# Pinning the pieces of a state-space set-up to places in a feed-forward layer

## The chip, the cores and the metric

The kernel runs on one core of a Trainium2 chip. The metric is device time in microseconds (us) for one execution. The engines are TensorE (PE in the profile: matmuls; PEld is its weight load), VectorE (DVE), ScalarE (ACT), GpSimd (POOL) and SyncE (SP), whose queue issues nearly all DMAs.

## The reference

One inference step of a two-layer decoder for 512 prompt tokens and 64 sample tokens, 576 columns in all. Layer 0 is dilated window attention and a gated feed-forward layer, layer 1 a state-space (S5) layer and another feed-forward layer. Cut to what the change is about:

```python
def swiglu(h, w_gate, w_up, w_down):
    return (jax.nn.silu(h @ w_gate) * (h @ w_up)) @ w_down

def ssm_layer(h, state0, w_in, a_re, a_im, log_dt, b_re, b_im, c_re, c_im, d_skip, w_glu):
    u = (h @ w_in).astype(f32)
    lam = lax.complex(a_re, a_im)
    dt = jnp.exp(log_dt)[:, None]
    abar = jnp.exp(lam * dt)
    bbar = ((abar - 1.0) / lam)[..., None] * lax.complex(b_re, b_im)
    cmat = lax.complex(c_re, c_im)
    ...   # scan over time: x = abar * x + bbar u; y = Re(C x) + D u
    g = jax.nn.gelu(y)
    val, gate = jnp.split(g @ w_glu, 2, axis=-1)
    return val * jax.nn.sigmoid(gate), h_last

x = x + out                       # mixer of the layer
x = x + swiglu(rmsnorm(x), ...)   # feed-forward of the layer
```

Everything in `ssm_layer` that doesn't depend on `h` (the powers of `abar`, `bbar`, and the matrices that turn eight time steps into one matmul) can be made ahead. That is the state-space set-up. The model width is 1024, the feed-forward width 2816, and there are 64 groups of 64 states.

## The kernel before

All matmuls are done as three: weights and activations are split into a high part that the matmul takes exactly and a low rest, and hi x hi, hi x lo and lo x hi are added. For each weight piece of 512 x 256, `fetch_w` (L85 to L89) loads it into one of four `raw` buffers, ScalarE makes `whi` (L99) and DVE makes `wlo = raw - whi` (L100), each with two buffers. `mark[0]` keeps the latest of these DVE instructions and `pem[0]` the latest matmul, as the code is traced. With every fetch, `pace` also issues one copy of a piece of the old key/value cache to the output, of about 1 MB (L83), and keeps these copies in program order on SyncE.

`ffn` (layer 0's feed-forward) works through the 2816 columns in three thirds of 4, 4 and 3 column blocks of 256. A column block takes a gate product (two weight pieces), the product with the norm on DVE (L1078), Silu on ScalarE, a second product with the norm on GpSimd (L1080, into `gt`), an up product (two pieces), and the product of both on DVE (L1085), which is split into `hh` and `hl`. After each third come four blocks of the down product, of two pieces each, added into `xT` (L1091). After each weight piece `gemm` calls `tick`. That takes the state-space set-up, a Python generator, one `yield` further. So `ffn` has 16 + 8, 16 + 8 and 12 + 8, or 68 places for it.

The set-up, `ssm_setup`, has these pieces (their places in the kernel before):

- loads of its constants (place 1), queued behind the last load of the output projection;
- on DVE: an exponential (3), sine and cosine (4, 5), the powers `Ar`, `Ai` (6), the factor `af` (8), `Bz` and four transposes on PE (10); then `at` is written to `a_scr` in device memory (12);
- on GpSimd: powers up to 63, `ee` (13 to 18), `E63` (21), written to `e_scr` (23);
- for each of eight families f: loads of `af` (from `a_scr`), `bt` and `C` (place 25 for f = 0); six products on GpSimd into `vx` (26 + 4f); four products on DVE for each half of `af` with `bt` (27 + 4f and 28 + 4f, L1513 to L1516); the write of `af` to `w_scr` (28 + 4f); the loads for f + 1, eight small matmuls into `aux`, DVE's copies into `kk`, and writes of `vx` (29 + 4f); the write of `kk` to `t_scr` (30 + 4f);
- loads of the finished constants `Wc`, `Ec`, `Tc`, `Vc` for families 0 to 3 (place 59).

A place is only where a piece stands in the program. The order on each engine is made by a planner, which simulates the whole program with durations of its own: an instruction whose inputs it takes to be there, and whose engine is free, goes into the order, and among several the one that stands first in the program. An engine then runs its list strictly in that order. So an instruction of a late place can stand ahead of one of an early place where the planner took the engine to be idle. Two things bind it: `tc.issue_after(i)` puts each instruction of its block that runs on `i`'s engine behind `i` in that engine's order, and `tc.keep_in_program_order` keeps such instructions of one engine in program order among themselves. Before the change the set-up uses the first for its constants' loads and for its matmuls on PE (behind `pem`), and the second not at all.

The tiles `af`, `bt`, `vx`, `kk` of the families have one buffer each, `C` two. The load of `af` for f + 1 so waits for the write of family f's `af` to `w_scr`. The pool of the families' tiles takes the place of the pool of `ee`, which in turn takes that of the first pieces.

Of the kernel before, what the change touches and what calls it, by code (L numbers as in the profile page):

```python
# [8 lines left out]
F32 = mybir.dt.float32  # L9
# [41 lines left out]
def _build(nc, tc, A, es):  # L51
# [51 lines left out]
    pem = [None]  # L103
# [943 lines left out]
def ffn(nc, tc, A, L, nin, nout, fill):  # L1047
# [20 lines left out]
    with ExitStack() as es:  # L1068
        hp = es.enter_context(pool("hp", bufs=9))
        wk = es.enter_context(pool("wkf", bufs=2))  # L1070
        for c0, c1 in THIRDS:
            h = {}
            for c in range(c0, c1):
                pg = gemm(lw("ffn_w_gate"), FF, range(KT), c * 256, nin.x)
                sg = []
                for m in range(2):
                    t = wk.tile([128, 2, HN], F32, name="gt")
                    v.tensor_tensor(t, pg[m][:, :, :HN], nin.r, OP.mult)  # L1078
# [197 lines left out]
def ssm_setup(nc, tc, A, L, keep, out):  # L1276
# [37 lines left out]
    with ExitStack() as es:  # L1314
# [7 lines left out]

        def cmul(eng, zr, zi, ar, ai, br, bi, t1, t2):
# [7 lines left out]
        with ExitStack() as e2:  # L1331
# [32 lines left out]
            g.memset(Bz, 0.0)  # L1364
            yield
            yield
            ar, ai = pc[:, 0], pc[:, 1]
            big = lambda name: wk.tile([128, 10, 32], F32, name=name)
            th, n, z, sn, cn = (big(x) for x in ("th", "n", "z", "sn", "cn"))
            lr, mag = wk.tile([128, 4, 32], F32, name="lr"), wk.tile([128, 4, 32], F32, name="mag")  # L1370
            ie = wk.tile([128, 4, 32], I32, name="ie")
            dt = tmp("dt")
            vexp(dt, pc[:, 2], n[:, 0], z[:, 0], sn[:, 0], ie[:, 0])
            v.tensor_tensor(lr[:, 0], ar, dt, OP.mult)
            v.tensor_tensor(th[:, 0], ai, dt, OP.mult)
            for k in range(1, 10):
                if k < 4:
                    v.tensor_scalar(lr[:, k], lr[:, 0], 2.0 ** k, None, op0=OP.mult)
                v.tensor_scalar(th[:, k], th[:, 0], 2.0 ** k, None, op0=OP.mult)
            fl = lambda x: x.rearrange("p a b -> p (a b)")  # L1380
            vexp(fl(mag), fl(lr), fl(n[:, :4]), fl(z[:, :4]), fl(sn[:, :4]), fl(ie))
            yield
            th, n, z, sn, cn = (fl(x) for x in (th, n, z, sn, cn))
            rnd(n, th, 1.0 / (2 * math.pi))
            for c in (6.28125, 0.0019350051879882812, 3.0199159819567874e-07):
                v.scalar_tensor_tensor(th, n, -c, th, op0=OP.mult, op1=OP.add)
            v.tensor_scalar(th, th, 0.5, None, op0=OP.mult)
            v.tensor_tensor(z, th, th, OP.mult)
            horner(sn, z, [(-1.0) ** k / math.factorial(2 * k + 1) for k in range(7, 0, -1)])
            v.scalar_tensor_tensor(sn, sn, 1.0, th, op0=OP.add, op1=OP.mult)  # L1390
            yield
            horner(cn, z, [(-1.0) ** k / math.factorial(2 * k) for k in range(8, 0, -1)])
            v.tensor_scalar(cn, cn, 1.0, None, op0=OP.add)
            v.tensor_tensor(th, sn, cn, OP.mult)
            v.tensor_scalar(th, th, 2.0, None, op0=OP.mult)
            v.tensor_tensor(z, sn, sn, OP.mult)
            v.tensor_scalar(z, z, -2.0, 1.0, op0=OP.mult, op1=OP.add)
            yield
            ui, ur = (x.rearrange("p (a b) -> p a b", b=32) for x in (th, z))
            v.memset(Ar[:, 0], 1.0)  # L1400
            v.memset(Ai[:, 0], 0.0)
            for k in range(4):
                v.tensor_tensor(Ar[:, 2 ** k], ur[:, k], mag[:, k], OP.mult)
                v.tensor_tensor(Ai[:, 2 ** k], ui[:, k], mag[:, k], OP.mult)
            two = wk.tile([128, 2, 512], F32, name="two")
            for m, n_ in ((2, 1), (4, 3)):
                w = slice(m + 1, m + 1 + n_)
                bc = lambda x: x[:, m:m + 1].to_broadcast([128, n_, 32])
                f1, f2 = (two[:, i, :n_ * 32].rearrange("p (m q) -> p m q", q=32) for i in range(2))
                cmul(v, Ar[:, w], Ai[:, w], Ar[:, 1:1 + n_], Ai[:, 1:1 + n_], bc(Ar), bc(Ai), f1, f2)  # L1410
            v.tensor_copy(rho, mag[:, 3])
            v.tensor_copy(U8[:, 0], ur[:, 3:10])
            v.tensor_copy(U8[:, 1], ui[:, 3:10])
            yield
            yield
            nr, den, fr, fi, t = tmp("nr"), tmp("den"), tmp("fr"), tmp("fi"), tmp("t")
            v.tensor_scalar(nr, Ar[:, 1], -1.0, None, op0=OP.add)
            ni = Ai[:, 1]
            v.tensor_tensor(den, ar, ar, OP.mult)
            v.tensor_tensor(t, ai, ai, OP.mult)  # L1420
            v.tensor_tensor(den, den, t, OP.add)
            v.reciprocal(den, den)
            v.tensor_tensor(fr, nr, ar, OP.mult)
            v.tensor_tensor(t, ni, ai, OP.mult)
            v.tensor_tensor(fr, fr, t, OP.add)
            v.tensor_tensor(fr, fr, den, OP.mult)
            v.tensor_tensor(fi, ni, ar, OP.mult)
            v.tensor_tensor(t, nr, ai, OP.mult)
            v.tensor_tensor(fi, fi, t, OP.subtract)
            v.tensor_tensor(fi, fi, den, OP.mult)  # L1430
            af = wk.tile([128, 8, 8, 2, 4], F32, name="af")
            fq = lambda x: x.rearrange("p (f q) -> p f q", q=4)[:, :, None, :].to_broadcast([128, 8, 8, 4])
            pw = lambda x: x[:, 0:8].rearrange("p s (f q) -> p f s q", q=4)
            cmul(v, af[:, :, :, 0], af[:, :, :, 1], pw(Ar), pw(Ai), fq(fr), fq(fi), *(two[:, i, :256].rearrange("p (f s q) -> p f s q", f=8, s=8) for i in range(2)))
            yield
            yield
            two = wk.tile([128, 2, 512], F32, name="two")
            b12 = [two[:, i].rearrange("p (a b) -> p a b", b=16) for i in range(2)]
            bc = lambda x: x[:, :, None].to_broadcast([128, 32, 16])
            for ri, (p, q, op) in enumerate(((fr, fi, OP.subtract), (fi, fr, OP.add))):  # L1440
                for i, x in enumerate((p, q)):
                    v.tensor_tensor(b12[i], bw[:, i], bc(x), OP.mult)
                for gl in range(2):
                    hs = slice(gl * 64, gl * 64 + 64)
                    v.tensor_tensor(Bz[hs, ri, :, gl], b12[0][hs], b12[1][hs], op)
            ps = aux.tile([128, 2, 512], F32, name="aux")
            with tc.issue_after(L["pem"][0].ins):
                for i in range(4):
                    te.transpose(ps[:, 0, i * 128:(i + 1) * 128], af.rearrange("p f s r q -> p (f s r q)")[:, i * 128:(i + 1) * 128], ident)
            at = wk.tile([128, 2, 512], F32, name="two")[:, 0].rearrange("p (a b) -> p a b", a=4)  # L1450
            s.activation(at, ps[:, 0].rearrange("p (a b) -> p a b", a=4), AF.Copy)
# [25 lines left out]
        with ExitStack() as e2:  # L1477
# [3 lines left out]

            def load(f):
                a = wk.tile([128, 2, 4, 128], F32, name="af")
                nc.sync.dma_start(a.rearrange("p r q c -> p (r q c)"), dram(scn["A"], f * 8192, [[0, 16], [1024, 8], [1, 1024]]))
# [8 lines left out]
            ab = load(0)  # L1493
            yield
            for f in range(8):
# [4 lines left out]
                a, af, bf, C = ab  # L1500
                cb = lambda i: C[:, i, :, None, :].to_broadcast(sh)
                pr, pi = pw(Ar), pw(Ai)
                g.tensor_scalar(C[:, 1], C[:, 1], -1.0, None, op0=OP.mult)
                for r, op in ((0, OP.add), (1, OP.subtract)):
                    g.tensor_tensor(vx[:, r], cb(r), pr, OP.mult)
                    g.tensor_tensor(vt_, cb(1 - r), pi, OP.mult)
                    g.tensor_tensor(vx[:, r], vx[:, r], vt_, op)
                yield
                for h in range(2):
# [3 lines left out]
                    v.tensor_tensor(t, x, b2(1), OP.mult)  # L1513
                    v.tensor_tensor(x, x, b2(0), OP.mult)
                    v.tensor_tensor(x[:, 0], x[:, 0], t[:, 1], OP.subtract)
# [346 lines left out]
```

## Time and profile before

| | |
|---|---|
| median of three runs | 1480.15 us (1478.9 to 1483.71) |
| the profiled execution: time / span of the core | 1485.73 us / 1483.9 us |
| mean granted clock of TensorE | 0.988 |
| feed-forward of layer 0, where the set-up's pieces stand | from about 423 to 875 us of the span |
| HBM read and written | 320.95 MB and 119.05 MB |
| DMA queue of SyncE and ScalarE (q1) | 317.93 MB, 62.6% of 16 engines |
| median time to landing: `raw<-ffn_w_down`, `raw<-ffn_w_gate`, cache copy of 1020 KB | 4.1, 5.8 and 7.8 us |

Line numbers such as L100 are those of the kernel. A row of a list of waits gives who waited, for whom, the sum in us, how often, and the longest. A row of a timeline gives the start in us from the start of the span, the duration, the engine, line and operation, the tile written and those read, and the count; idle time before it, with what ended it, stands in brackets. "SPq" is the issue of a DMA by SyncE; "DMA to landing" is the time from issue to the last byte. Times of the trace are one execution's, so sums made from them are measured against its own 1485.73 us.

### The profile page before, as it was taken

The page shows a single profiled execution, that of the slowest core. Times are in us where ns is not written, and L with a number is a line of the kernel's source. Part 1 is how long each engine was busy: PE and PEld are TensorE (multiplying, and loading weights), DVE is VectorE, ACT ScalarE, POOL GpSimd, SP SyncE. Part 2 cuts the span into 40 slices and gives each one's busy share as a digit, 9 for nine tenths or more (in the row PEclk, how much of TensorE's full clock was granted, in tenths as well). Part 3 has the DMA queues.
Part 4 walks back from the last instruction along what each step waited for, and adds up shares of the span by engine and source line. Part 5 has one row for each costly group of instructions (what it writes and reads, how often), then busy time and mean ns, then how long its engine had stood idle before and what let it go on. Part 6 is the DMA issues. An engine that isn't in the chain of part 4 may idle for free. (4 is left out here: it accounts for less than half of the span.)

```text
span 1483.9 us, 29688 instructions
## 1 busy us (share of the span) xinstructions
PE 1428.0 (96%) x12307; PEld 1335.4 (90%) x12307; DVE 958.2 (65%) x1512; ACT 588.8 (40%) x955; POOL 338.9 (23%) x416
## 2 busy tenths in 40 slices
PE   9999999999989996999999999699999999999998
PEld 7888777777889996999999999689999999999998
DVE  5898989745599344464545567756586646745762
ACT  4534455465542221222122363434375424532541
POOL 2022232320123573064443131131010001100110
PEclk9999999999999998999999999899999999999999
DMA  7566788989965859989999947864267857775532
GB/s 247 206 237 232 231 308 263 367 302 341 317 227 214 303 182 348 353 284 361 334 341 324 324 135 226 269 172 138 86 160 192 244 211 186 184 239 158 144 106 64
DMA packets 185767, 354.65 MB, mean 239 GB/s; under 512 B 31936, under 2 KB 120256, under 8 KB 184224
## 3 DMA queue, kind: packets, MB, share of 16 engines
q1 hardware_dynamic: 172896, 317.93, 62.6%
q0 software_dynamic: 9968, 32.12, 9.7%
q10 hardware_dynamic: 2768, 2.70, 0.5%
q8 instruction: 97, 1.59, 0.4%
q14 instruction: 38, 0.31, 0.1%
HBM read 320.95 MB, written 119.05 MB: 297 GB/s over the span
## 5 line engine op out<-in xcount | busy, mean ns | idle before, releaser
L108 PE MATMUL acc<-xgh,wlo 128*128 128x288 f32 x1056 | 226.9, 297 | 4.2 <-DVE wlo L100 4.2
L108 PE MATMUL acc<-xgh,whi 128*128 128x288 f32 x1056 | 227.9, 297 | 1.6 <-DVE xgl L1567 0.8
L108 PE MATMUL acc<-xgl,whi 128*128 128x288 f32 x1056 | 227.5, 297 | 0.0
L99 ACT ACTIVATE whi<-raw 128x1024 fp32r<-128x1024 f32 x98 | 102.0, 1041 | 265.5 <-PE acc L108 237.8
L100 DVE TENSOR_TENSOR wlo<-raw,whi 128x1024 fp32r<-128x1024 f32 x98 | 130.2, 1329 | 102.5 <-ACT whi L99 100.6
L1171 PE MATMUL bank<-xoh,whi 128*128 128x288 f32 x616 | 183.1, 297 | 5.4 <-ACT cq L1182 4.1
L1171 PE MATMUL bank<-xoh,wlo 128*128 128x288 f32 x616 | 182.4, 296 | 0.2 <-DVE wlo L1113 0.2
L1171 PE MATMUL bank<-xol,whi 128*128 128x288 f32 x616 | 182.4, 296 | 0.0
L108 PEld LDWEIGHTS acc<-xgh,wlo 128*128 128x128 f32 x1056 | 170.4, 189 | 5.4 <-DVE wlo L100 5.1
L108 PEld LDWEIGHTS acc<-xgh,whi 128*128 128x128 f32 x1056 | 170.2, 189 | 3.6 <-issue 2.1
L108 PEld LDWEIGHTS acc<-xgl,whi 128*128 128x128 f32 x1056 | 170.7, 189 | 0.3
L1171 PEld LDWEIGHTS bank<-xoh,whi 128*128 128x128 f32 x616 | 116.3, 189 | 6.9 <-ACT cq L1182 5.2
L1113 DVE TENSOR_TENSOR wlo<-raw,whi 128x1024 fp32r<-128x1024 f32 (+1 forms) x57 | 70.3, 1233 | 77.8 <-ACT whi L1112 76.7
L384 PE MATMUL acc<-whi,xh 128*128 128x512 f32 x288 | 118.7, 414 | 1.4 <-ACT xh L324 1.3
L1171 PEld LDWEIGHTS bank<-xoh,wlo 128*128 128x128 f32 x616 | 116.5, 189 | 0.6 <-DVE wlo L1113 0.6
L1171 PEld LDWEIGHTS bank<-xol,whi 128*128 128x128 f32 x616 | 116.4, 189 | 0.1
L1112 ACT ACTIVATE whi<-raw 128x1024 fp32r<-128x1024 f32 (+1 forms) x57 | 58.4, 1029 | 140.0 <-DMA raw<-ffn_w_down 65.3
L384 PE MATMUL acc<-wlo,xh 128*128 128x512 f32 x288 | 112.2, 391 | 0.0
L384 PE MATMUL acc<-whi,xl 128*128 128x512 f32 x288 | 111.5, 393 | 0.0
L108 PE MATMUL acc<-hh,wlo 128*128 128x288 f32 x352 | 76.8, 300 | 11.7 <-DVE wlo L100 11.7
L108 PE MATMUL acc<-hh,whi 128*128 128x288 f32 x352 | 76.9, 300 | 0.0
L1127 POOL DMA_DIRECT2D s<-w_gu x22 | 19.4, 883 | 250.4 <-DMA s<-w_gu 91.2
(424 smaller groups left out, 3028.4 us busy)
## 6 DMA issues: line engine op xcount, KB each, us to landing
o_kv_s<-cache_kv_w SPq DMA_DIRECT2D x64, 1020.0 KB, 7.8
kc<-cache_kv_w SPq DMA_DIRECT2D x100, 512.0 KB, 6.8
raw<-ffn_w_down SPq DMA_DIRECT2D x40, 512.0 KB, 4.1
raw<-w_qkv SPq DMA_DIRECT2D x36, 512.0 KB, 7.4
raw<-w_gu SPq DMA_DIRECT2D x33, 512.0 KB, 3.4
kc<-qscr SPq DMA_DIRECT2D x32, 512.0 KB, 6.3
o_kv_s<-cache_kv_w SPq DMA_DIRECT2D x16, 1008.0 KB, 7.9
raw<-ffn_w_gate SPq DMA_DIRECT2D x22, 512.0 KB, 5.8
```

Source lines behind the costliest of these rows:

```text
L99: s.activation(hi, raw, AF.Copy)
L100: mark[0] = v.tensor_tensor(lo, raw, hi.bitcast(F32), OP.subtract)
L108: pem[0] = te.matmul(ps[:, c, :HN], w, x[:, c * HN:(c + 1) * HN], start=first and i == 0, stop=last and i == 2)
L384: ins = nc.tensor.matmul(*a, **kw)
L1112: s.activation(hi, raw, AF.Copy)
L1113: v.tensor_tensor(lo, raw, hi.bitcast(F32), OP.subtract)
L1127: g.dma_start(fl(t), block(c, m, k), accum_op=OP.add)
L1171: tc.keep_in_program_order(te.matmul(acc[q][:, :HN], a[:, k, i * 128:(i + 1) * 128], nin.x[x, k][b], skip_group_check=n != "a12", start=n ...
```

## The change

The set-up's DVE instructions from the exponential on are traced inside `later()`, which is `issue_after` of the latest weight split at that place. GpSimd's products of a family are put behind the latest gate product (`gmark`). The first piece comes one place later, and with it all that follow. A family's products, GpSimd's and both halves on DVE, come in one place, 28 + 4f, with the write to `w_scr`; the load of `C` for f + 1 comes one place behind that, those of `af` and `bt` two places, the matmuls and the writes of `vx` three. The loads are kept in program order on SyncE, where only the cache copies and the loads of the output projection were so kept. The set-up ends at place 60. No arithmetic is changed.

```diff
-    pem = [None]
+    pem, gmark = [None], [None]
...
                     s.activation(t, t, AF.Silu)
-                    g.tensor_tensor(t, t, nin.r, OP.mult)
+                    L["gmark"][0] = g.tensor_tensor(t, t, nin.r, OP.mult)
...
+        def later(m="mark"):
+            return tc.issue_after(L[m][0].ins)
...
             g.memset(Bz, 0.0)
-            yield
-            yield
-            ar, ai = pc[:, 0], pc[:, 1]
+            for _ in range(3):
+                yield
+            with later():
+                ar, ai = pc[:, 0], pc[:, 1]
...
+            with later():
+                th, n, z, sn, cn = (fl(x) for x in (th, n, z, sn, cn))
...
+            with later():
+                horner(cn, z, [(-1.0) ** k / math.factorial(2 * k) for k in range(8, 0, -1)])
...
+            with later():
+                ui, ur = (x.rearrange("p (a b) -> p a b", b=32) for x in (th, z))
...
+            with later():
+                nr, den, fr, fi, t = tmp("nr"), tmp("den"), tmp("fr"), tmp("fi"), tmp("t")
...
+            with later():
+                two = wk.tile([128, 2, 512], F32, name="two")
...
+            kept = tc.keep_in_program_order
+
             def load(f):
                 a = wk.tile([128, 2, 4, 128], F32, name="af")
-                nc.sync.dma_start(a.rearrange("p r q c -> p (r q c)"), dram(scn["A"], f * 8192, [[0, 16], [1024, 8], [1, 1024]]))
+                kept(nc.sync.dma_start(a.rearrange("p r q c -> p (r q c)"), dram(scn["A"], f * 8192, [[0, 16], [1024, 8], [1, 1024]])))
                 b = wk.tile([128, 2, 4, 128], F32, name="bt")
-                nc.sync.dma_start(b.rearrange("p r q c -> p (r q c)"), dram(A["s_bt"], f * 16384, [[1024, 16], [0, 8], [1, 1024]]))
+                kept(nc.sync.dma_start(b.rearrange("p r q c -> p (r q c)"), dram(A["s_bt"], f * 16384, [[1024, 16], [0, 8], [1, 1024]])))
+                return a, fl(a), fl(b)
+
+            def load_c(f):
                 c = wk.tile([128, 2, 4, 16], F32, name="C", bufs=2)
-                nc.sync.dma_start(c, A["s_c"][:, :, f * 4:f * 4 + 4])
-                return a, fl(a), fl(b), c
+                kept(nc.sync.dma_start(c, A["s_c"][:, :, f * 4:f * 4 + 4]))
+                return c
...
-            ab = load(0)
+            ab, C = load(0), load_c(0)
+            yield
             yield
             for f in range(8):
...
-                g.tensor_scalar(C[:, 1], C[:, 1], -1.0, None, op0=OP.mult)
-                for r, op in ((0, OP.add), (1, OP.subtract)):
-                    g.tensor_tensor(vx[:, r], cb(r), pr, OP.mult)
-                    g.tensor_tensor(vt_, cb(1 - r), pi, OP.mult)
-                    g.tensor_tensor(vx[:, r], vx[:, r], vt_, op)
-                yield
+                with later("gmark"):
+                    g.tensor_scalar(C[:, 1], C[:, 1], -1.0, None, op0=OP.mult)
+                    for r, op in ((0, OP.add), (1, OP.subtract)):
+                        g.tensor_tensor(vx[:, r], cb(r), pr, OP.mult)
+                        g.tensor_tensor(vt_, cb(1 - r), pi, OP.mult)
+                        g.tensor_tensor(vx[:, r], vx[:, r], vt_, op)
                 for h in range(2):
...
-                    v.tensor_tensor(t, x, b2(1), OP.mult)
-                    v.tensor_tensor(x, x, b2(0), OP.mult)
-                    v.tensor_tensor(x[:, 0], x[:, 0], t[:, 1], OP.subtract)
-                    v.tensor_tensor(x[:, 1], x[:, 1], t[:, 0], OP.add)
-                    if h:
-                        nc.sync.dma_start(scn["W"][f], a)
-                    yield
+                    with later():
+                        v.tensor_tensor(t, x, b2(1), OP.mult)
+                        v.tensor_tensor(x, x, b2(0), OP.mult)
+                        v.tensor_tensor(x[:, 0], x[:, 0], t[:, 1], OP.subtract)
+                        v.tensor_tensor(x[:, 1], x[:, 1], t[:, 0], OP.add)
+                nc.sync.dma_start(scn["W"][f], a)
+                yield
+                if f < 7:
+                    C = load_c(f + 1)
+                yield
                 if f < 7:
                     ab = load(f + 1)
+                yield
                 pk = aux.tile([128, 2, 512], F32, name="aux")
...
-            yield
         consts(0, nc.sync)
```

More of the change, by code (lines that the diff above doesn't have):

```diff
@@ L1384, in ssm_setup @@
[L1384 to L1390, printed above, removed]
-            yield
@@ L1401, in ssm_setup @@
[L1401 to L1410, printed above, removed]
@@ L1434, in ssm_setup @@
-            cmul(v, af[:, :, :, 0], af[:, :, :, 1], pw(Ar), pw(Ai), fq(fr), fq(fi), *(two[:, i, :256].rearrange("p (f s q) -> p f s q", f=8, s=8) for i in range(2)))
-            yield
-            yield
[L1437 to L1451, printed above, removed]
+            with later():
+                two = wk.tile([128, 2, 512], F32, name="two")
+                b12 = [two[:, i].rearrange("p (a b) -> p a b", b=16) for i in range(2)]
+                bc = lambda x: x[:, :, None].to_broadcast([128, 32, 16])
+                for ri, (p, q, op) in enumerate(((fr, fi, OP.subtract), (fi, fr, OP.add))):
+                    for i, x in enumerate((p, q)):
+                        v.tensor_tensor(b12[i], bw[:, i], bc(x), OP.mult)
+                    for gl in range(2):
+                        hs = slice(gl * 64, gl * 64 + 64)
+                        v.tensor_tensor(Bz[hs, ri, :, gl], b12[0][hs], b12[1][hs], op)
+                ps = aux.tile([128, 2, 512], F32, name="aux")
+                with tc.issue_after(L["pem"][0].ins):
+                    for i in range(4):
+                        te.transpose(ps[:, 0, i * 128:(i + 1) * 128], af.rearrange("p f s r q -> p (f s r q)")[:, i * 128:(i + 1) * 128], ident)
+                at = wk.tile([128, 2, 512], F32, name="two")[:, 0].rearrange("p (a b) -> p a b", a=4)
+                s.activation(at, ps[:, 0].rearrange("p (a b) -> p a b", a=4), AF.Copy)
```

109 lines of the change are left out of this document (61 added, 48 removed).

## The prediction

> **What bounds the kernel now.** I read the page first, then the waits of TensorE, then stretches of the timeline, engine by engine, wherever a wait was long. From the page:
>
> ```profile
> span 1483.9 us, 29688 instructions
> PE 1428.0 (96%) x12307; PEld 1335.4 (90%) x12307; DVE 958.2 (65%) x1512; ACT 588.8 (40%) x955; POOL 338.9 (23%) x416
> ```
>
> TensorE (PE) is the bound: it is idle for only 1483.9 - 1428.0 = 55.9 us. A change that leaves the matmuls alone can win no more than that, plus what a slow clock costs after an idle time. Who causes the idle time, from the list of PE's waits (sum, times, longest):
>
> ```profile
> PE acc L108 <- DVE wlo L100: 16.9, 6, 11.7
> PE acc L1605 <- DMA U<-u_scr: 12.7, 1, 12.7
> ```
>
> The second lies in the state-space layer itself, which the change doesn't touch. The first lies in the feed-forward layer before it, whose weight splits (`wlo`) share VectorE (DVE) with the set-up's pieces. Its longest wait, in PE's timeline (start, duration, what; in brackets the idle time):
>
> ```profile
> 570.48 0.43 PE L108 MATMUL acc<-hh,whi 128*128 128x288 f32 x2
> 570.75 0.42 PE L108 MATMUL acc<-hl,whi 128*128 128x288 f32 x2
> 582.88 0.85 PE L108 MATMUL acc<-hh,wlo 128*128 128x288 f32 x2 [11.71 <-DVE wlo L100]
> 588.32 0.60 PE L108 MATMUL acc<-hl,whi 128*128 128x288 f32 x2
> 588.76 0.42 PE L108 MATMUL acc<-hh,wlo 128*128 128x288 f32 x2
> ```
>
> After 11.71 us of waiting, PE also runs slowly: 12 pairs lie between 582.88 and 588.76, at 5.88 us. At 570.75 - 570.48 = 0.27 us a pair they would take 3.2, so 2.7 us more are lost: 14.4 together. The Trainium skill ("TensorE: Matmul & The Clock Gate", What's actually happening) has the clock at half rate until about 3.4 us of sustained work have passed. By that figure the loss would be an estimated 1.7 us instead of 2.7 and the sum below 1 us smaller; the trace shows 5.88 slow microseconds, and I keep it.
>
> What stood ahead of `wlo`, from the timelines of DVE, ScalarE and SyncE's queue:
>
> ```profile
> 558.71 1.23 DVE L100 TENSOR_TENSOR wlo<-raw,whi 128x1024 fp32r<-128x1024 f32 x1
> 571.22 0.69 DVE L1513 TENSOR_TENSOR wt<-af,bt 128x512 f32<-128x512 f32 x1 [11.28 <-DMA Ec<-e_scr]
> 576.02 1.59 DVE L1514 TENSOR_TENSOR af<-af,bt 128x512 f32<-128x512 f32 x1
> 580.41 2.41 DVE L100 TENSOR_TENSOR wlo<-raw,whi 128x1024 fp32r<-128x1024 f32 x1
> ```
>
> ```profile
> 557.62 1.07 ACT L99 ACTIVATE whi<-raw 128x1024 fp32r<-128x1024 f32 x1 [5.34 <-PE acc L108]
> 564.01 1.06 ACT L99 ACTIVATE whi<-raw 128x1024 fp32r<-128x1024 f32 x1 [5.33 <-PE acc L108]
> ```
>
> ```profile
> 494.84 0.37 SPq L1454 DMA_DIRECT2D a_scr<-two  x1
> 549.50 0.68 SPq L1474 DMA_DIRECT2D e_scr<-ee  x1
> 558.21 0.57 SPq L1484 DMA_DIRECT2D af<-a_scr  x1
> ```
>
> The high half was ready at 565.1, but DVE runs in order and already stood at family 0's first multiplication, which waited until 571.22 for tiles that were asked for only at 558.21. Then eight multiplications ran, 9.2 us up to 580.41, and only then the split. So the cost is a wrong order on DVE with a late transfer at its head. A second, smaller place is where the set-up begins; PE's waits between 400 and 500 us, then its timeline:
>
> ```profile
> PE acc L108 <- DVE wlo L100: 2.8, 3, 1.4
> PE aux L206 <- POOL ssum L199: 1.3, 1, 1.3
> PE acc L108 <- DVE z L1340: 0.7, 1, 0.7
> ```
>
> ```profile
> 434.27 1.53 PE L206 MATMUL aux<-ssum,ones 128*128 128x288 f32 x4 [1.34 <-POOL ssum L199]
> 438.63 0.42 PE L108 MATMUL acc<-xgh,wlo 128*128 128x288 f32 x2
> ```
>
> All of these, 2.8 + 1.3 + 0.7 = 4.8 us, lie before 435 us. From 434.27 to 438.63 there are 17 matmuls, at 4.36 us instead of 17 x 0.133 = 2.3: 2.1 us of slow clock. Front together: 6.9 us.
>
> **The change, part by part.** A "place" is one call of `tick`, one weight piece of 6.4 us on PE (564.01 - 557.62).
>
> *First piece at place 4 instead of 3, pinned.* Its exponential now stands behind the split of piece 4, which is made while PE does piece 3, at about 436 us. In the profile it starts at 405.90, in the middle of the output projection:
>
> ```profile
> 405.90 1.41 DVE L1348 TENSOR_SCALAR sn<-pc 128x32 f32<-128x32 f32 x1 [1.88 <-DMA xr<-x_scr]
> 408.04 1.16 DVE L100 TENSOR_TENSOR wlo<-raw,whi 128x1024 fp32r<-128x1024 f32 x1
> ```
>
> ```profile
> 403.48 1.04 ACT L99 ACTIVATE whi<-raw 128x1024 fp32r<-128x1024 f32 x1
> ```
>
> The split at 408.04 had its high half at 404.5 and DVE idle until 405.90; only the order kept it back. DVE by stretches (length; PE, PEld, DVE, ACT, POOL busy; clock; DMA):
>
> ```profile
> 405.90:437.00 31.10, 26.15 (x177) 24.49 (x176) 30.79 (x82) 12.95 (x17) 12.29 (x7) 0.97 0.67 244
> 437.00:479.50 42.50, 42.50 (x316) 42.50 (x315) 39.64 (x97) 14.66 (x18) 13.44 (x4) 0.98 0.61 223
> 475.00:500.00 25.00, 25.00 (x191) 25.00 (x190) 13.48 (x17) 6.32 (x9) 2.85 (x2) 1.00 0.85 303
> ```
>
> In the first stretch DVE is full and PE loses 5 of 31 us; in the second DVE is 93% full with set-up work and PE loses nothing; in the third DVE has 11.5 us free in 25. So the work that leaves the first stretch goes to where DVE stays full for some 15 to 20 us longer, and PE has been fed there at the same load. I take the front's 6.9 us as gone, with 1 us given back; bounds of that cost: 0 (the second stretch) and 6.9 (the first stretch repeated later).
>
> *Everything after it one place later.* The write of `a_scr` hangs on transposes that already stood behind a place's last matmul, so it moves 6.4 us back against PE's work; with the front's 6.9 us gone it leaves at about the same time, 494.84. The chain behind it (powers on GpSimd, `e_scr`, `af`) keeps its times, about 571 for the landing. Cost: nothing, hidden under the margin that comes next; without it, 6.4 us of lateness.
>
> *Family 0 pinned at place 28, loads at place 26.* Pieces 25 and 26 are the gate weights of column block 4, whose last product with the norm tells when PE ends them:
>
> ```profile
> 610.79 0.76 DVE L1078 TENSOR_TENSOR gt<-acc,rstd 128x576 f32<-128x576 f32 x1 [2.28 <-PE acc L108]
> ```
>
> So piece 26 ends at about 611, or 589 if all of PE's waits go; the split of piece 28 follows within 2.3 us. Margin to the landing: 591 - 571 = 20 us. No load can now hold up splits 23 and 24: gain 14.4 us. What is late next? PE had no other wait there.
>
> *Families 1 to 7 pinned every fourth place.* The pin is a lower bound on the place only. What must fit in 4 x 6.4 + 2.3 = 27.9 us: the split (2.3), a family's multiplications, the write of `w_scr` (the load overwrites the same tile), the load. Clean, a half takes 0.69 + 0.69 + 0.42 + 0.42, the family 4.4 us:
>
> ```profile
> 600.70 0.69 DVE L1514 TENSOR_TENSOR af<-af,bt 128x512 f32<-128x512 f32 x1
> 601.42 0.42 DVE L1515 TENSOR_TENSOR af<-af,wt 128x256 f32<-128x256 f32 x1
> ```
>
> ```profile
> L1518 SPq DMA_DIRECT2D w_scr<-af x8: 344/410/534, 580.5 to 823.8; - x8
> DMA to landing us min/median/max: 3.5/6.5/11.3
> ```
>
> ```profile
> L1484 SPq DMA_DIRECT2D af<-a_scr x8: 562/582/1083, 558.2 to 802.4; - x8
> DMA to landing us min/median/max: 5.9/8.6/13.4
> ```
>
> By medians 2.3 + 4.4 + 6.5 + 8.6 = 21.8, which fits with 6 us to spare. With DVE at its slowest (9.2) and both landings at their maxima it is 36.2: 8.3 late. Even then DVE may wait 12.8 - 1.3 - 2.3 - 4.4 = 4.8 us (two pieces, less the next split's own time, the split and the family before it) until the next split is late for PE. I cost it 1 us in all, between 0 and 7 x 1.25 (next row). One more wait goes, when a half-family stood ahead of a split:
>
> ```profile
> 645.30 0.54 PE L108 MATMUL acc<-xgh,wlo 128*128 128x288 f32 x2 [1.25 <-DVE wlo L100]
> ```
>
> *GpSimd behind the gate product, `C` two places ahead.* GpSimd's products of family f no longer come before the gate product of their own column block; and they start, now as before, only when PE has read the last family's:
>
> ```profile
> 630.64 3.39 POOL L1505 TENSOR_TENSOR vx<-C,Ar 128x576 f32<-128x576 f32 x2 [16.45 <-PE aux L1526]
> ```
>
> PE has no wait with the gate product as its cause, so this gains 0.
>
> *Loads kept in program order on SyncE.* Every cache copy of place 31 + 4f now stands behind load f + 1, which waits for a landing. So copies come in bursts, and weight loads queue behind the waiting instruction. The longest such block before, among SyncE's waits:
>
> ```profile
> SPq L1474 <- POOL E L1471: 14.2, 1, 14.2
> ```
>
> A weight load stood behind it (the next on SyncE's queue), and PE's next wait is only that of 570.75, which has another cause. The new block is a landing of `w_scr`, 11.3 at most. Cost 0.
>
> **Sum**: 14.4 + 6.9 + 1.25 = 22.6 gained, 2 given back: 20.6. The profiled execution took 1485.73 us (span 1483.9) and would take 1465.1; the median of the three runs is 1480.15, which gives **1459.5**.
>
> **The rivals.**
>
> *A: the front's waits move along with the work* (17%). DVE is as full after 437 as before it, and a pinned chain has no other chain to interleave with. Against it: the second stretch above. Gain 14.4 + 1.25, time 1464.5.
>
> *B: DVE and GpSimd collide* (12%). One place now holds all eight multiplications and GpSimd's six products. The row at 576.02 took 1.59 us against 0.69 at 600.70, with GpSimd's products running beside it, and the wait at 645.30 is what a family in collision cost PE: 1.25 us. At eight families that is 10, so with A's loss half in, 1480.15 - 22.6 + 10 + 3 = 1470.5. The Trainium skill ("SBUF — State Buffer", Who interferes with whom) says that a DVE instruction with two SBUF inputs and a reading GpSimd instruction exclude each other for a whole instruction; by that rule, which the two durations bear out, B comes about if they do meet. Against it: GpSimd waits for PE's read of the last family, one piece after DVE's start.
>
> *C: it doesn't do what it says* (3%). If the chain to `af` slips by more than the 20 us margin, family 0 blocks a later split instead, and with A's loss beside it only the 1.25 us are won: 1478.9, within 0.3%.
>
> *D, slower: each family's load is late* (8%). Place: DVE's queue at pieces 32, 36 and so on. At the maxima above a load is 8.3 us late; PE then waits 8.3 - 4.8 = 3.5 and loses 2.7 of clock, 6.2 x 7 = 43: 1480.15 - 22.6 + 43 = 1500. It decides from 3.9 us a family, (22.6 + 4.4) / 7. For it: landings reach these maxima when copies come in bursts. Against it: the medians leave 6 us.
>
> **How the numbers follow.** My forecast has 60%, A 17, B 12, C 3, D 8. The least that runs of this kernel tell from no change is about 0.3%, 4.4 us. Faster by more: 60 + 17 + 12 = 89, less 2 for a B that grows, 87%; same 3 + 2 = 5%; slower 8%. The range goes from all 22.6 us gained plus the runs' own spread (3.5), 1454, to B with its collisions at a half more, 1475; outside lie most of C and D, and little below.
>
> **What would show it.** Right: no PE wait over 2 us between 400 and 880 us, no clock below 1 near 580; the first exponential after 430 us; family 0's first multiplication behind a split and not idle before. Step by step: a DVE idle time ended by `af` or `bt` speaks for D, multiplications of 1.4 to 1.6 us for B, PE waits on `wlo` between 437 and 500 us for A. What would make the whole wrong: a new order elsewhere in the kernel, since one plan covers it all; a wait at `u_scr` longer than 12.7 us would be the first sign.

## The result and the profile after

The changed kernel takes 1465.68 us (median of 4 runs, 1464.36 to 1467.69), the kernel before beside it 1479.53 (4 runs, 1478.22 to 1483.71): ratio 0.9903, 95% interval 0.9880 to 0.9926. That is 13.9 us faster; 20.6 were forecast. The time lies inside the range, 6.2 us above the point. The profiled execution took 1467.69 us (span 1465.9, mean clock 0.994).

The page of after, busy time, share and instructions of each engine:

```profile
PE 1424.9 (97%) x12307; PEld 1332.2 (91%) x12307; DVE 969.5 (66%) x1512; ACT 588.4 (40%) x955; POOL 330.9 (23%) x416
```

TensorE's idle time fell from 55.9 to 1465.9 - 1424.9 = 41.0 us; its busy time for the same matmuls fell by 3.1, at a mean granted clock of 0.994 instead of 0.988. VectorE, with as many instructions as before, got 11.3 us *busier*. That is the trace of what the change costs. By stretches of the span (start:end, length; busy us of PE, PEld, DVE, ACT, POOL with their counts; clock; DMA share; GB/s), before:

```profile
423.00:500.00 77.00, 73.88 (x536) 72.86 (x536) 62.64 (x149) 27.62 (x34) 21.88 (x9) 0.98 0.69 244
500.00:600.00 100.00, 88.29 (x644) 88.06 (x643) 43.48 (x41) 18.98 (x20) 59.21 (x75) 0.93 0.79 273
600.00:700.00 100.00, 98.75 (x774) 97.42 (x773) 54.82 (x66) 25.52 (x29) 43.53 (x28) 1.00 0.95 328
```

and after:

```profile
423.00:500.00 77.00, 77.00 (x577) 76.79 (x576) 66.12 (x166) 26.92 (x32) 14.11 (x8) 1.00 0.68 245
437.00:479.50 42.50, 42.50 (x321) 42.50 (x320) 41.61 (x129) 13.20 (x16) 7.95 (x4) 1.00 0.61 223
500.00:600.00 100.00, 100.00 (x753) 100.00 (x752) 41.78 (x40) 21.79 (x23) 54.70 (x72) 1.00 0.80 286
600.00:700.00 100.00, 97.42 (x757) 95.45 (x756) 70.61 (x73) 24.85 (x29) 46.09 (x33) 1.00 0.99 344
```

The stretches up to 600 us are now full, at full clock: the front's waits and family 0's long wait are gone. In that from 600 to 700 TensorE is busy 1.3 us less than before, and VectorE 15.8 us more. TensorE's timeline of after has three waits between 423 us and the end of the feed-forward, 3.05 us in all:

```profile
605.61 0.53 PE L108 MATMUL acc<-xgh,wlo 128*128 128x288 f32 x2 [1.73 <-DVE wlo L100]
...
692.59 0.54 PE L108 MATMUL acc<-hh,wlo 128*128 128x288 f32 x2 [0.85 <-DVE wlo L100]
...
798.51 0.53 PE L108 MATMUL acc<-xgh,wlo 128*128 128x288 f32 x2 [0.47 <-DVE wlo L100]
```

What stood ahead of the split that the first of them waited for, in VectorE's timeline of after (family 0's eight products are L1529 to L1532):

```profile
591.47 1.22 DVE L100 TENSOR_TENSOR wlo<-raw,whi 128x1024 fp32r<-128x1024 f32 x1
592.61 1.92 DVE L1529 TENSOR_TENSOR wt<-af,bt 128x512 f32<-128x512 f32 x1
594.56 0.69 DVE L1530 TENSOR_TENSOR af<-af,bt 128x512 f32<-128x512 f32 x1
595.29 1.34 DVE L1531 TENSOR_TENSOR af<-af,wt 128x256 f32<-128x256 f32 x1
596.55 1.45 DVE L1532 TENSOR_TENSOR af<-af,wt 128x256 f32<-128x256 f32 x1
598.03 1.61 DVE L1529 TENSOR_TENSOR wt<-af,bt 128x512 f32<-128x512 f32 x1
599.67 1.80 DVE L1530 TENSOR_TENSOR af<-af,bt 128x512 f32<-128x512 f32 x1
601.50 1.35 DVE L1531 TENSOR_TENSOR af<-af,wt 128x256 f32<-128x256 f32 x1
602.78 1.64 DVE L1532 TENSOR_TENSOR af<-af,wt 128x256 f32<-128x256 f32 x1
604.35 1.21 DVE L100 TENSOR_TENSOR wlo<-raw,whi 128x1024 fp32r<-128x1024 f32 x1
```

and beside it GpSimd's, in after:

```profile
592.20 1.78 POOL L1080 TENSOR_TENSOR gt<-gt,rstd 128x576 f32<-128x576 f32 x1 [1.78 <-ACT gt L1079]
593.96 0.81 POOL L1519 TENSOR_SCALAR C<-C 128x64 f32<-128x64 f32 x1
594.75 1.60 POOL L1521 TENSOR_TENSOR vx<-C,Ar 128x576 f32<-128x576 f32 x1
596.31 1.41 POOL L1522 TENSOR_TENSOR vt<-C,Ai 128x576 f32<-128x576 f32 x1
597.68 1.41 POOL L1521 TENSOR_TENSOR vx<-C,Ar 128x576 f32<-128x576 f32 x1
599.06 1.86 POOL L1523 TENSOR_TENSOR vx<-vx,vt 128x576 f32<-128x576 f32 x1
601.00 1.57 POOL L1522 TENSOR_TENSOR vt<-C,Ai 128x576 f32<-128x576 f32 x1
602.65 1.49 POOL L1523 TENSOR_TENSOR vx<-vx,vt 128x576 f32<-128x576 f32 x1
...
622.40 1.51 POOL L1522 TENSOR_TENSOR vt<-C,Ai 128x576 f32<-128x576 f32 x1
625.21 2.88 POOL L1521 TENSOR_TENSOR vx<-C,Ar 128x576 f32<-128x576 f32 x2 [1.30 <-PE aux L1545]
```

No transfer is late: the family is not waited for, it is slow. It takes 604.35 - 592.61 = 11.7 us instead of a clean 4.4, with GpSimd's gate product and then its six family products running beside it. VectorE's four groups of family products in after (busy us, mean ns behind the bar):

```profile
L1529 DVE TENSOR_TENSOR wt<-af,bt 128x512 f32<-128x512 f32 x16 | 20.3, 1268 | 0.2
L1530 DVE TENSOR_TENSOR af<-af,bt 128x512 f32<-128x512 f32 x16 | 17.4, 1086 | 0.5
L1531 DVE TENSOR_TENSOR af<-af,wt 128x256 f32<-128x256 f32 x16 | 15.9, 994 | 0.4
L1532 DVE TENSOR_TENSOR af<-af,wt 128x256 f32<-128x256 f32 x16 | 15.1, 941 | 0.0
```

They sum to 68.7 us; before, the same four (L1513 to L1516) took 16.2 + 14.1 + 11.7 + 10.2 = 52.2. Family by family, the eight products sum to 11.8, 9.7, 9.7, 9.1, 5.5, 9.7, 8.7 and 4.4 us in after, so six of the eight families run beside GpSimd's work. The kernel before had such families too (0, 2 and 4, at 9.3, 9.7 and 8.6).

**The balance of the profiled pair.** By the first matmul of each stage in TensorE's timeline, output projection to feed-forward took 28.13 us before and 25.68 after, the feed-forward (up to the state-space layer's first matmul with `U`) 478.5 and 460.5, and the rest, up to the end of the last matmul, 578.4 and 578.5. The two stages give 2.45 + 18.0 = 20.45 us, for which the forecast had 20.6. The attention ahead of them, where nothing is changed, ended 2.3 us later in the execution of after; so the spans differ by 18. In the medians it is 13.9: the execution of before that I worked from, 1485.73 us, is slower than all four runs beside the result. (Beside the later runs the same kernel's median was 1482.2 to 1485.4 us; it is those four that were quick.)

### The profile page after: what moved, and what is told of

Its sections match the earlier page's. It is cut to its first block, busy times and chain, and to the rows that moved or that the text cites. A ratio compares the mean times of both kernels' runs of the same rounds, so it can differ in the third digit from the quotient of the medians.

```text
span 1465.9 us, 29677 instructions
## 1 busy us (share of the span) xinstructions
PE 1424.9 (97%) x12307; PEld 1332.2 (91%) x12307; DVE 969.5 (66%) x1512; ACT 588.4 (40%) x955; POOL 330.9 (23%) x416
## 5 line engine op out<-in xcount | busy, mean ns | idle before, releaser
L100 DVE TENSOR_TENSOR wlo<-raw,whi 128x1024 fp32r<-128x1024 f32 x98 | 126.8, 1294 | 88.2 <-ACT whi L99 85.6
```

What stands on the lines that cost most here:

```text
L100: mark[0] = v.tensor_tensor(lo, raw, hi.bitcast(F32), OP.subtract)
```

## The experiments

My theory at this point: (1) the pin on the families' VectorE products takes the long wait away, whose length hangs on when the loads land; (2) the front's part is won in full; (3) something in the families' part, the pin on GpSimd or the crowded place, makes the two engines meet and gives some 3 us back. Rivals: the gain comes from one part alone; the loads' kept order costs; the crowded place costs whatever GpSimd does. The ratios are to the kernel before on the same chip, "feed-forward" is the time from its first matmul to the state-space layer's first with `U` in the profiled execution, and "waits" are TensorE's in that stage.

| run | median us | before beside it | ratio, 95% interval | feed-forward us | waits us |
|---|---|---|---|---|---|
| e1_before | 1484.60 | 1482.59 | 1.0009 (0.9994 to 1.0025) | 475.8 | 13.9 |
| e2_front | 1475.25 | 1482.59 | 0.9944 (0.9924 to 0.9964) | 472.8 | 10.3 |
| e3_families | 1472.44 | 1482.59 | 0.9926 (0.9904 to 0.9948) | 465.3 | 5.9 |
| e4_after | 1467.62 | 1482.59 | 0.9895 (0.9869 to 0.9920) | 462.1 | 3.1 |
| e5_no_gmark | 1462.82 | 1485.42 | 0.9861 (0.9825 to 0.9897) | 458.0 | 0.3 |
| e6_no_kept | 1468.77 | 1485.42 | 0.9892 (0.9861 to 0.9923) | 461.7 | 3.1 |
| e7_unpinned | 1477.56 | 1485.42 | 0.9946 (0.9926 to 0.9966) | 470.5 | 9.1 |
| e8_apart | 1463.21 | 1485.42 | 0.9867 (0.9840 to 0.9895) | 459.0 | 1.3 |
| e9_after | 1466.74 | 1483.60 | 0.9884 (0.9863 to 0.9904) | 461.8 | 3.1 |
| e10_no_gmark | 1464.05 | 1483.60 | 0.9861 (0.9836 to 0.9886) | 457.7 | 0.3 |
| e11_apart_no_gmark | 1461.86 | 1483.60 | 0.9856 (0.9836 to 0.9876) | 458.3 | 0.5 |
| e12_one_earlier | 1460.72 | 1482.19 | 0.9861 (0.9839 to 0.9883) | 458.4 | 1.3 |

**The kernel before, again (no edit).**

> The kernel before, once more. Own theory: the wait at family 0's place hangs on when its loads land, so it differs from execution to execution, and the profiled one (1485.73 us against a median of 1479.53) had a long one: a second profile near 1479.5 us should show that wait at 5 to 9 us instead of 11.7, with the front's waits unchanged at 4 to 5 us. Rival: the wait is 11 to 12 us again and the 6 us between the profiled execution and the median lie elsewhere (in the attention layer, or spread).

Its long wait, in TensorE's timeline, and what VectorE stood at:

```profile
579.83 0.85 PE L108 MATMUL acc<-hh,wlo 128*128 128x288 f32 x2 [7.90 <-DVE wlo L100]
```

```profile
568.14 0.69 DVE L1513 TENSOR_TENSOR wt<-af,bt 128x512 f32<-128x512 f32 x1 [7.45 <-DMA C<-s_c]
```

Same place, same cause, but 7.90 us instead of 11.71: the multiplication began 3.1 us sooner, at 568.14 instead of 571.22, when the last load had landed, and TensorE came to the wait 0.8 us later, at 571.93 instead of 571.17. With 2.7 us of slow clock behind it (twelve pairs again, 579.83 to 585.76) the wait costs 10.6 us, not 14.4. So its length moves with the landing. Which of the two lengths is the usual one, this profile doesn't show: at 1480.95 us it is the second fastest of this run's twelve executions (1480.65 to 1488.38). That the landing makes the times of executions differ, the runs suggest without settling it: the 17 of the kernel before on this chip spread over 10.8 us, e4's of the change over 0.8, but e9's, on another chip, over 6.5.

**The front alone**: the first pieces pinned and one place later, families as in the kernel before (this diff and the ones below are against the change).

```diff
-            ab, C = load(0), load_c(0)
-            yield
+            ab = load(0)
...
-                with later("gmark"):
...
+                yield
                 for h in range(2):
...
-                    with later():
```

> Only the set-up's pieces up to the write of a_scr are pinned and come one place later; the families are as before. Own theory: the front's waits before 435 us (4.8 us and 2.1 us of slow clock) go and nothing comes back, so 5 to 7 us are gained, about 1473 us, and the wait at family 0 stays or shifts. Rival A (the waits move along with the work): gain under 2 us, with PE waits on wlo between 437 and 500 us.

7.3 us faster (5.3 to 11.3 by the interval), with no wait of TensorE left between 400 and 500 us: the front's 6.9 are won and nothing is given back. (The run changes pins and places of the front together; which of the two does it, no run separates.) Family 0's wait stays, now in two pieces (list of TensorE's waits from 500 to 883 us):

```profile
PE acc L108 <- DVE xT L1091: 5.9, 1, 5.9
PE acc L108 <- DVE wlo L100: 4.4, 2, 3.6
```

The first has another name, but the same cause: the down product's addition, which frees a bank, stands behind the same blocked multiplication. With the slow pairs behind each (572.73 to 577.22 and 582.31 to 587.28, 2.1 and 2.3 us over 0.27 us a pair) the two cost 13.8 us, near the 14.4 of the first profile.

**The families alone**: the first pieces as before the change, none of them pinned up to `Bz`, and all of the families' part.

```diff
-            for _ in range(3):
-                yield
-            with later():
+            yield
+            yield
...
```

> Only the families are changed (products, loads, order); the first pieces are unpinned and in their old places. Own theory: the wait at family 0 goes and up to 3 us of collisions between VectorE and GpSimd come in, while the front's 4.8 us of waits stay: 6 to 11 us gained, 1469 to 1473 us. Rival: if the wait at family 0 were 14.4 us in every execution, the gain would be 11 to 13 us, 1467 to 1468 us. The two parts alone should add up to the whole change's gain of about 14 us within 2 us.

10.2 us faster (7.7 to 14.2). That fits e1's 10.6 plus the 1.25, less the 1.1 us of waits that stay; with 14.4 in place of 10.6 it would be about 14.5, just outside the interval. The front's waits are all there. The two parts' ratios multiply to 0.987, the whole has 0.9895 on the same chip: they add up within the intervals, at most with a little lost. That little is taken up below: with the families alone, their products on VectorE sum to 49.8 us, not 68.7.

**The change again (no edit), twice.**

> The changed kernel once more, on the chip of the other three. Own theory: 1464 to 1467 us, the same small PE waits on wlo at families 0, 3 and 7 (together 2 to 4 us), since their order is fixed and no landing ends them. Rival: those waits come and go with the landings of af and bt, and differ by more than 2 us from the first profile.

> The changed kernel once more, as the measure for the two runs beside it. Own theory: 1466 to 1468 us, about 13 to 18 us under the kernel before. In the feed-forward layer's time up to 880 us TensorE waits for wlo about 3 us in all, the longest near 606 us with 1.7 us.

Both times the same three waits at the same places (the third is behind family 6, not 7). The collision is part of the order, not chance. The times, 1467.62 and 1466.74 us, are 15.0 and 16.9 us under the kernel before beside them, a little more than in the first result.

**GpSimd not pinned.**

```diff
-                with later("gmark"):
+                with ExitStack():
```

> The changed kernel without the pin of GpSimd's family products behind the gate product. Own theory: that pin buys nothing, since the products also wait for PE's read of the last family: within 2 us of the changed kernel (1464 to 1468 us), no new PE wait over 2 us. Rival: unpinned products come ahead of the gate product, which then comes late for the up product: PE waits of 3 us and more, 1470 us or above.

> The changed kernel with GpSimd's six products of a family no longer pinned behind the gate product, all else as in the change. Theory 'the pin on GpSimd puts its products beside VectorE's, and each slows the other': GpSimd's products of family 0 run near 567 us, VectorE's eight are clean, waits for wlo below 0.5 us, and the time is 2 to 5 us under the changed kernel of the same chip. Rival 'the small waits come from the crowded place alone': waits stay at 2 to 3 us and the time is that of the changed kernel within 1 us.

In both runs GpSimd makes family 0's products at about 569 to 578, long before VectorE's at 592, the sums fall to 53.1 and 53.9 us, and of the waits 0.3 us is left. The first of these products, in GpSimd's timeline of e5:

```profile
569.14 1.22 POOL L1521 TENSOR_TENSOR vx<-C,Ar 128x576 f32<-128x576 f32 x1
```

So the pin that I priced at nothing, in the prediction and again ahead of e5, has a price. Between e10 and e9, on the same chip, the medians differ by 2.7 us, the feed-forward by 4.1.

**Loads not kept in program order.**

```diff
-            kept = tc.keep_in_program_order
+            kept = lambda i: i
```

> The changed kernel with its family loads not kept in program order on SyncE. Own theory: they are issued about as early as before, since a landing and not the order holds them; within 2 us of the changed kernel, family 0's af at about 558 us. Rival: the order is what brings the loads in time; without it a load comes late, VectorE idles over 4 us ahead of a family's first product and PE waits 3 us or more, 1470 us or above.

Waits and feed-forward are those of the change: the kept order neither wins nor costs anything that can be measured here.

**VectorE's family products not pinned.**

```diff
-                    with later():
+                    with ExitStack():
                         v.tensor_tensor(t, x, b2(1), OP.mult)
```

> The changed kernel with the pin taken off the families' eight products on VectorE alone; places, loads and all other pins stay. Own theory: the pin is what removes the long wait: without it the planner again puts family 0 ahead of an earlier split, and PE waits 6 to 12 us near 570 us: 1473 to 1480 us. Rival: the later place and the earlier loads do it by themselves: 1464 to 1468 us, no PE wait over 3 us.

The waits come back, 9.1 us in all, though not as one at family 0: they are spread over families 0 to 2. Two of them in TensorE's timeline, and VectorE at the head of family 0 and of family 1:

```profile
570.32 0.53 PE L108 MATMUL acc<-hh,whi 128*128 128x288 f32 x2 [2.79 <-DVE xT L1091]
...
609.65 0.80 PE L108 MATMUL acc<-xgh,wlo 128*128 128x288 f32 x2 [2.51 <-DVE wlo L100]
```

```profile
568.18 0.69 DVE L1529 TENSOR_TENSOR wt<-af,bt 128x512 f32<-128x512 f32 x1 [8.16 <-DMA Ec<-e_scr]
...
599.10 1.43 DVE L1529 TENSOR_TENSOR wt<-af,bt 128x512 f32<-128x512 f32 x1 [3.15 <-DMA bt<-s_bt]
```

VectorE idles at the head of a family until a load lands, and a split waits behind it. (At family 1 GpSimd runs beside it as well: its eight products sum to 9.4 us.) Loads two places ahead don't prevent that; the pin does. (1) is shown in so far as the pin is needed; whether it would be enough without the earlier loads, no run tests.

**GpSimd one place behind VectorE.** The empty place ahead of family 0 is taken out, and GpSimd's products move behind the `yield` that follows the write to `w_scr`.

```diff
-            yield
             for f in range(8):
...
-                with later("gmark"):
...
                 nc.sync.dma_start(scn["W"][f], a)
                 yield
+                with later("gmark"):
+                    g.tensor_scalar(C[:, 1], C[:, 1], -1.0, None, op0=OP.mult)
...
```

> The changed kernel with VectorE's family products one place earlier (27 + 4f) than GpSimd's (28 + 4f), the loads one place earlier and the matmuls at 30 + 4f. Own theory: the 3 us of small PE waits left in the feed-forward layer come from both engines working on one family at once (13 us for eight products instead of 4.4); apart, those waits fall below 1 us and 2 to 4 us are gained over the changed kernel: 1462 to 1464 us where that has 1466 to 1467. Rival: the waits come from the split standing behind eight products of any length, or the products meet the gate product instead: 1465 to 1468 us.

> GpSimd's products moved one place behind VectorE's (loads one place earlier), and not pinned either. Theory of the collision: nothing is left to win once GpSimd runs ahead of VectorE by itself, so the time is that of the run without the pin within 1.5 us. Rival 'distance between the two is what counts, and the two edits add up': another 2 to 4 us below the run without the pin. A third way: the loads one place earlier find the write to w_scr not done, SyncE's queue is held, and the time is 1 to 4 us above the run without the pin.

With the pin, the sum falls to 49.8 us and the waits to 1.3; without it as well, 51.9 and 0.5. That doing both wins more than one alone is not shown: e11's median is 2.2 us below e10's, more than the 1.5 I had allowed, but the intervals overlap, and in the feed-forward, where the edits act, e11 is 0.6 us longer. But e8 changed two things, GpSimd's place and the family's. The last run separates them.

**All families one place earlier, GpSimd pinned and beside VectorE in the program as in the change.**

```diff
             ab, C = load(0), load_c(0)
             yield
-            yield
             for f in range(8):
```

> The changed kernel with one empty place taken out ahead of family 0, so that all families (products, loads, matmuls) come one place earlier, as in the run with the families' part alone; GpSimd stays pinned and in the same place as VectorE. Own theory 'the place decides whether VectorE's products stand ahead of the column block's gate product or right behind it, where GpSimd starts too': the eight products of family 0 stand ahead of or around the gate product and are mostly clean, the families' products on VectorE sum to 50 us instead of 69, TensorE's waits for wlo in the feed-forward fall from 3.1 to about 1.1 us, and the time is 2 to 4 us under that of the change, near 1463. Rival 'the pin on GpSimd alone makes the collision, wherever the place': products still sum to 65 us or more, waits stay at 3 us, and the time is 1466 to 1468.

VectorE's timeline of e12 (L1528 to L1531 are the products, L1078 the gate product with the norm), and GpSimd's first product of the family:

```profile
585.57 0.68 DVE L1528 TENSOR_TENSOR wt<-af,bt 128x512 f32<-128x512 f32 x1
586.29 0.69 DVE L1529 TENSOR_TENSOR af<-af,bt 128x512 f32<-128x512 f32 x1
586.89 0.75 DVE L1078 TENSOR_TENSOR gt<-acc,rstd 128x576 f32<-128x576 f32 x1
...
592.13 1.21 DVE L100 TENSOR_TENSOR wlo<-raw,whi 128x1024 fp32r<-128x1024 f32 x1
```

```profile
594.97 1.22 POOL L1520 TENSOR_TENSOR vx<-C,Ar 128x576 f32<-128x576 f32 x1
```

The product groups of e12:

```profile
L1529 DVE TENSOR_TENSOR af<-af,bt 128x512 f32<-128x512 f32 x16 | 17.5, 1095 | 0.4
L1528 DVE TENSOR_TENSOR wt<-af,bt 128x512 f32<-128x512 f32 x16 | 13.5, 843 | 2.5 <-DMA bt<-s_bt 2.3
L1530 DVE TENSOR_TENSOR af<-af,wt 128x256 f32<-128x256 f32 x16 | 10.4, 649 | 0.2
L1531 DVE TENSOR_TENSOR af<-af,wt 128x256 f32<-128x256 f32 x16 | 8.8, 547 | 0.0
```

Sum 50.2 us, waits 1.3, and at 1460.72 us the lowest median of the study (its ratio, 0.9861, is that of e5 and e10). One `yield` decides it for families 0 to 2, which now take 5.5 us each. One place earlier, VectorE's products begin while TensorE still works on the column block's gate; the gate products, behind which GpSimd is pinned, come in their midst, and GpSimd's first product of the family starts at 594.97, when VectorE is through and has gone on to the next split (592.13). One place later, they begin right behind the second gate product, when GpSimd begins too. So for these families neither the pin nor the crowded place is enough; it takes the pin **and** the later place. That is also why e3, which has the pin but not the shift, had none there. The one place doesn't free every family. Family 3 still meets GpSimd in e12, in VectorE's and in GpSimd's timeline:

```profile
670.60 1.91 DVE L1528 TENSOR_TENSOR wt<-af,bt 128x512 f32<-128x512 f32 x1
```

```profile
672.71 1.61 POOL L1520 TENSOR_TENSOR vx<-C,Ar 128x576 f32<-128x576 f32 x1
```

Its products sum to 10.6 us (10.6 in e3, 9.7 in e8), and the only wait left in e12, 1.29 us at 683.63, is that of the split behind them.

How much it costs: feed-forward stages are 460.5 to 462.1 us in the four profiles of kernels in which the two meet at families 0 to 2 (the change three times, e6), and 457.7 to 459.0 in the five in which they meet there little or not at all (e5, e8, e10, e11, e12): about 3 us by the means. The ratios are 0.9884 to 0.9903 against 0.9856 to 0.9867, about 5 us by the means, with single intervals that overlap. Which of the versions without the meeting is best can't be told from these runs; that they beat the kernel before is plain, and that they beat the change is likely, since all five ratios lie below all four.

## Why the prediction was right, and where its sizes were off

- **The long wait goes**: right, and shown by e3 and e7. **Its size, 14.4, is the doubtful term.** It was that of one execution, and for that execution the sum held: the two stages gave 20.45 us where 20.6 were forecast, and the profiled execution after took 1467.69 us where 1465.1 were forecast, of which 2.3 came about in the attention. In e1 the same wait costs 10.6, in e2 13.8, and e3's gain is 10.2. The error was to take a wait that ends with a landing off a median that lay 5.6 us below its execution: up to 3.8 of the 6.7 us missing. How long the wait was in the executions that make that median, no run shows. Part of the 6.7 may also be the four quick runs: e4 and e9 put the change's gain at 15.0 and 16.9.
- **The front, 6.9 won, 1 given back**: right in mechanism, and nothing was given back. Between 437 and 479.5 us VectorE is busy 41.61 of 42.50 us and TensorE loses nothing. The first exponential, in VectorE's timeline of after, starts behind its split:

```profile
439.38 1.22 DVE L100 TENSOR_TENSOR wlo<-raw,whi 128x1024 fp32r<-128x1024 f32 x1
440.51 1.40 DVE L1351 TENSOR_SCALAR sn<-pc 128x32 f32<-128x32 f32 x1
```

  Rival A is out: no wait between 437 and 500 us in any run with the front's part.
- **"Everything after it one place later", with "Cost: nothing"**: wrong. I followed only the chain to the landing, and that part held (`af` was asked for at 556.1). The shift also moved the families against the gate products. That GpSimd's pin "gains 0" overlooked that it can cost something. Together they cost 1.5 to 4.4 us of the feed-forward (the nearest and farthest profiles above).
- **Families, 1 us lost**: 3.05 us of waits. Rival B came true in mechanism, at a third of its price of 10. Against it I had said that GpSimd waits for TensorE's read of the last family. Family 0 has no family before it, and the longest wait, 1.73 us, is behind family 0. For the next families the wait comes too late and holds too little: in after, VectorE starts family 1 at 620.17, GpSimd's first product, into `vt`, runs ahead of the wait at 622.40, and the others start at 625.21, 5 us after VectorE, while its eight last until 629.93. Families 1 and 2 still take 9.7 us each; the argument didn't hold for them either.
- **D, late loads**: out. In the result's profile VectorE has no idle time that ends with `af` or `bt` (in e4's one of 0.26 us); the landings of `af` and of the write to `w_scr` were at most 10.3 and 7.5 us, below the 13.4 and 11.3 of before. With the order kept on SyncE these landings got no longer.
- **Kept loads, 0**: right (e6). **C**: out.

Of the 6.7 us, up to 3.8 are the long wait's size and 3.05 - 1 = 2 the families'; the front gave 1 more than forecast. The other 1.9 or more no run here can tell from chance: the part behind the feed-forward, which the change doesn't touch, took between 574 and 580 us in the profiles.

## What to carry to other kernels

A wait that ends with a transfer's landing can differ by some us from execution to execution (11.71 and 7.90 here). Take its size from more than one profile before subtracting it from a median of other executions. When pieces are pinned to places, look at each pair of engines that work there, not only at each engine's own order: a shift by one place that is harmless to every single queue can put two engines' products on top of each other. "It waits for the one before" keeps two engines apart only if the wait ends after the other engine is done, and only for the instructions that stand behind it.

## What the runs showed of the hardware

- VectorE's and GpSimd's products took turns, instruction by instruction. In the two timelines of after at family 0, each VectorE product but the second ends a fixed time after a GpSimd product: those of 512 elements 0.55 us (593.98 and 594.53, 599.09 and 599.64, 600.92 and 601.47), those of 256 elements 0.28 (596.35 and 596.63, 597.72 and 598.00, 602.57 and 602.85, 604.14 and 604.42), each sum start plus duration. So the recorded 1.34 to 1.92 us read as waiting and then work: beside an idle GpSimd the same shapes take 0.69 and 0.42. The Trainium skill ("SBUF — State Buffer", Who interferes with whom) says that a VectorE instruction with two SBUF inputs contends with a GpSimd instruction that reads SBUF, and calls the shared ports an exclusive lock. The trace agrees, and adds the pattern: one VectorE product for one GpSimd product in family 0, which made 11.7 us of a family of 4.4.
- A wait's length doesn't settle whether TensorE's clock falls behind it. After waits of 1.73 us (605.61 in after) and 2.79 (570.32 in e7) the pairs (two matmuls, one row of the timeline) go on at 0.27 us; after 2.51 (609.65 in e7) they are slow for 3.5 us, after 3.21 (640.98 in e7) for 3.0, after 3.57 and 5.87 (e2) for 5.0 and 4.5, after 7.90 and 11.71 for 5.9. The Trainium skill ("TensorE: Matmul & The Clock Gate", What's actually happening) has the full clock back after about 3.4 us of sustained work; the slow phases here, 3.0 to 5.9 us, lie on both sides of that.
